# A transformer block on one Trainium2 core: the last matrix product cut into chunks of 3, 3, 3 and 2 tiles

## The chip, the cores and the metric

The kernel runs on one core of one Trainium2 chip. It is timed as device microseconds of one execution. The five engines of the core are called PE (TensorE, the matrix products), DVE (VectorE), ACT (ScalarE), POOL (GpSimd) and SP (SyncE, which here only issues DMAs). Each engine works through its own list of instructions in a fixed order; an instruction that waits holds up everything behind it on the same engine.

## The reference

One layer: banded attention and a Fourier branch in parallel, merged, then a gated ConvFFN. Every sub-layer has an RMS norm before and after it and a residual. The change touches the ConvFFN alone, which is

```python
def conv_ffn(h, w_up, conv_w, conv_b, w_down):
    u, gate = jnp.split(h @ w_up, 2, axis=-1)
    up = jnp.pad(u, ((0, 0), (1, 1), (0, 0)))
    u = up[:, :-2] * conv_w[0] + up[:, 1:-1] * conv_w[1] + up[:, 2:] * conv_w[2] + conv_b
    return (jax.nn.silu(u) * gate) @ w_down
...
x = x + gt2 * rmsnorm(conv_ffn(h2, ...), g_post2)
```

with 1024 tokens, width 1024 and a hidden width of 2816, which is 22 tiles of 128. All is float32.

## The kernel before

**Products.** A float32 operand is split into a rounded high part (an ACT copy) and the rest (a DVE subtraction); a product is then three matmuls (`mm3`: high·high, high·low, low·high). The blocks of a 2x2 block matrix product are formed by Winograd's seven products P1 to P7. A "pair" is one such 2x2 product. Its results collect in three PSUM banks: P1, P6, P7 and P4 run one after another through bank X, P5 and then P3 through Y, P2 in Z. Between P1, P6, P7 and P4 ACT copies X out (`sn`), and the next product into X waits for that copy. P3 adds to Y, so that it waits until what P7's evacuation needs of Y (block 22) has been read by DVE.

**Order.** `wino_items` lists all products ("items") of the stage: for each pair P1, P2, then P4 and P3 of the pair before, then P6, P5, P7. The ConvFFN has 266 items: 22 up pairs (u0 to u21, 84 matmuls each), then 16 down pairs. `run2` walks the list; before the matmuls of item k it emits hooks, `ahead` (loads up to 9 items ahead; high parts 4, low parts 3 items ahead) and `flush` (what was put off to item k by `at_item`). So the place of each instruction on each engine is fixed by these numbers. Item 155 is the product P3 of the last up pair u21, item 156 the P6 of the first down pair d00.

**Down.** The 11 K tiles of each half of w_down are cut into chunks `CH`: 2, 3, 3 and 3 tiles. A chunk has four pairs, one for each m (two token tiles, m and m+4); pair d13 is chunk 1, m = 3. A product of a chunk of 3 is 9 matmuls, of a chunk of 2 it is 6. The sums over chunks stay in SBUF tiles `yd[i, n]`. `d_prep` brings the seven moving operands of the next chunk during the chunk before: w_down loads on SP's queue at items i0-7 to i0+3 (i0 is P1 of the last pair of the chunk before), ACT copies and DVE subtractions from i0-4 on, differences on POOL. The stationary operands of P1, P2 and P4 are stored split by the up stage (`READY`); those of P3, P5, P6 and P7 are stored whole and split in the down stage.

**Evacuation.** In chunks 1 to 3 DVE first adds the bank to the copy (`add(sn, sn, pst)`), and POOL adds the result to `yd`. In the last chunk each finished tile is squared on ACT, gated on POOL (`d_gate`), and with both halves there follow a root on ACT (`rstd_steps`) and a scale and residual on DVE (`d_out`) and the store. The last five products are written out by hand with a chain of its own for each of the last two token tiles.

**Loads.** A load into a two-part operand takes two SBUF tiles of a pool of 40 (`s`); SP waits where a tile is still in use, and each DMA waits for the eighth before it.

Of the kernel before, what the change touches and what calls it, by code (L numbers as in the profile page):

```python
# [16 lines left out]
P = 128  # L17
D = 1024
# [22 lines left out]
def block_kernel(ctx: ExitStack, tc: tile.TileContext, t: dict, out: bass.AP, dbg: dict):  # L41
# [166 lines left out]
    def wino(pairs, items, psf, hooks, FETCH=0):  # L208
# [9 lines left out]
        def do_fetch(j, p):  # L218
            ld, _, nm, _, nk = pairs[j]
            parts = ld[p]  # L220
            names = (f"h{p}_{nm}", f"l{p}_{nm}") if len(parts) == 2 else (f"r{p}_{nm}",)
            ts_ = [s(n, R if len(parts) == 2 else F)[:, :nk * P] for n in names]
            for x, src in zip(ts_, parts):
                load(out=fbits(x) if len(parts) == 2 else x, in_=src)
            st[j][p if len(parts) == 2 else STA[p]] = tuple(ts_) if len(parts) == 2 else ts_[0]
# [1460 lines left out]
    def d_prep(c, jl):  # L1686
# [25 lines left out]
        at(i0 - 7, lambda: ld("11", 0, 0))  # L1712
        at(i0 - 5, lambda: ld("21", 1, 0))
        at(i0 - 4, lambda: ld("12", 0, 1))
        at(i0 - 2, lambda: ld("22", 1, 1))
        at(i0 + 3, lambda: ld("21b", 1, 0))
# [30 lines left out]
    def d_out(i, n, r):  # L1747
        nc.vector.scalar_tensor_tensor(out=yd[i, n], in0=yd[i, n], scalar=r, in1=x1t[i, n], op0=ALU.mult, op1=ALU.add)  # L1748
# [321 lines left out]
```

## Time and profile before

| | us |
|---|---|
| median of 3 runs | 1413.59 (1411.74 to 1414.54) |
| the profiled execution | 1413.6 |
| its span, first to last instruction | 1411.8 |
| PE busy | 1285.2 (91%) |
| DVE busy | 1111.7 (79%) |
| ACT busy | 685.0 (49%) |
| POOL busy | 650.1 (46%) |

A matmul of the stage starts about 0.23 us after the one before it while PE has its full clock of 2.4 GHz, and about 0.43 us after it at 1.2 GHz. "Idle before" in a row of PE is the wait ahead of that matmul, and the arrow names what ended it. A count (x111) in a stretch of 25 us is that of the instructions that lie in it, those at its two edges included.

### The profile page before, as it was taken

How to read it: one execution, taken by the hardware profiler on the slowest of the kernel's cores; microseconds unless marked ns; L12 is line 12 of the kernel's file. 1: busy time of each engine (PE TensorE's matmuls, PEld its weight loads, DVE VectorE, ACT ScalarE, POOL GpSimd, SP SyncE). 2: the span in 40 equal slices, each digit the busy share in tenths (PEclk: the TensorE clock that was granted, in tenths of full speed). 3: DMA queues.
4: the chain of work that ended last, by engine and by line, in shares of the span. 5: the costliest groups of instructions: out<-in, count | busy, mean ns of one | idle time of the engine just before them, and what ended most of it. 6: DMA issues, size and time to landing. Idle time of an engine off the chain costs nothing. (4 is left out here: it accounts for less than half of the span.)

```text
span 1411.8 us, 18488 instructions
## 1 busy us (share of the span) xinstructions
PE 1285.2 (91%) x5840; PEld 1040.8 (74%) x5840; DVE 1111.7 (79%) x1768; ACT 685.0 (49%) x1414; POOL 650.1 (46%) x480
## 2 busy tenths in 40 slices
PE   4769979887999999999987999999999997999995
PEld 3658858666888887778766888888888875777774
DVE  6887999998688897663899986666666696777987
ACT  7555333323566776332755554444544464443442
POOL 1673554554044335430476554444444444364754
PEclk8779999998999999999999999999999999999997
DMA  9714768674614444741622444444344558657563
GB/s 305 220 53 144 227 211 277 199 240 136 201 41 120 123 125 120 233 170 53 189 65 68 134 139 130 119 116 123 108 124 129 153 154 256 213 181 223 164 214 135
DMA packets 253303, 223.63 MB, mean 158 GB/s; under 512 B 15100, under 2 KB 206228, under 8 KB 253204
## 3 DMA queue, kind: packets, MB, share of 16 engines
q1 hardware_dynamic: 253204, 222.44, 51.7%
q8 instruction: 46, 0.75, 0.2%
q14 instruction: 53, 0.43, 0.1%
HBM read 165.49 MB, written 56.62 MB: 157 GB/s over the span
## 5 line engine op out<-in xcount | busy, mean ns | idle before, releaser
L68 DVE TENSOR_TENSOR lP_u<-A_u,hP_u 128x512 fp32r<-128x512 f32 x132 | 103.1, 784 | 43.3 <-ACT hP_u L292 24.4
L354 ACT COPY snP_u<-X_u 128x512 f32<-128x512 f32 x57 | 33.5, 588 | 142.3 <-PE X_u L87 122.9
L68 POOL TENSOR_TENSOR A_u<-A_u,A_u 128x512 f32<-128x512 f32 x44 | 72.3, 1645 | 37.1 <-issue 22.3
L1245 POOL TENSOR_SCALAR p<-p,sm 128x640 f32<-128x640 f32 (+1 forms) x64 | 48.5, 777 | 84.3 <-PE pp L1250 39.2
L68 POOL TENSOR_TENSOR yd<-yd,snP_d 128x512 f32<-128x512 f32 x33 | 52.1, 1579 | 75.7 <-DVE snP_d L68 75.5
L68 POOL TENSOR_TENSOR A_u<-S_u,A_u 128x512 f32<-128x512 f32 x22 | 29.5, 1342 | 102.7 <-DVE lP_u L68 102.4
L292 ACT CAST hP_u<-A_u 128x512 fp32r<-128x512 f32 x121 | 74.6, 619 | 0.9 <-DVE u L68 0.9
L68 DVE TENSOR_TENSOR lP_d<-rP_d,hP_d 128x384 fp32r<-128x384 f32 (+1 forms) x64 | 55.7, 873 | 7.1 <-ACT hP_d L292 6.8
L354 ACT COPY snP_d<-X_d 128x512 f32<-128x512 f32 x46 | 26.8, 584 | 64.3 <-PE X_d L87 55.7
L80 ACT CAST ph<-pp 128x512 fp32r<-128x512 f32 x76 | 44.3, 585 | 22.5 <-PE pp L1250 21.3
L68 DVE TENSOR_TENSOR pl<-pp,ph 128x512 fp32r<-128x512 f32 x76 | 51.6, 680 | 3.1 <-ACT ph L80 2.6
L719 DVE SCALAR_TENSOR_TENSOR acc<-wm,sv,acc 128x512 f32<-128x512 f32 x56 | 51.2, 915 | 1.1 <-DMA wm<-in_w_mod 0.3
L1239 ACT ACTIVATE p<-p,nm 128x640 f32<-128x640 f32 (+1 forms) x64 | 51.3, 802 | 0.7 <-DVE nm L1232 0.7
L1555 POOL TENSOR_SCALAR z<-xr,ry 128x512 f32<-128x512 f32 x15 | 16.7, 1121 | 74.5 <-DVE ry L68 68.0
L1225 DVE CUSTOM_DVE_ANT_0 p<-ss,mask 128x640 f32<-128x640 f32 (+1 forms) x64 | 49.9, 780 | 0.0
L1250 PE MATMUL pp<-ident,p 128*128 128x128 f32 x304 | 46.9, 274 | 3.1 <-POOL p L1245 1.8
L68 POOL TENSOR_TENSOR wd<-wd,wd 128x512 f32<-128x512 f32 x22 | 35.2, 1618 | 27.7 <-DMA wd<-in_w_down 16.1
L68 DVE TENSOR_TENSOR lP_g<-A_g,hP_g 128x512 fp32r<-128x512 f32 x48 | 44.4, 934 | 4.2 <-ACT hP_g L80 3.9
L85 PE MATMUL X_d<-dT,hP_d 128*128 128x512 f32 x88 | 36.5, 414 | 12.0 <-ACT snP_d L354 11.9
L635 ACT ACTIVATE c_g<-c_g 128x512 f32<-128x512 f32 x32 | 19.8, 631 | 56.4 <-DVE c_g L68 48.2
L68 DVE TENSOR_TENSOR u<-Y_u,snP_u 128x512 f32<-128x512 f32 x22 | 15.2, 689 | 39.9 <-PE Y_u L87 39.9
L1250 PEld LDWEIGHTS pp<-ident,p 128*128 128x128 f32 x304 | 37.1, 140 | 12.4 <-POOL p L1245 3.6
(860 smaller groups left out, 4816.1 us busy)
## 6 DMA issues: line engine op xcount, KB each, us to landing
A_u<-in_w_up SPq DMA_DIRECT2D x88, 256.0 KB, 3.8
wm<-in_w_mod SPq DMA_DIRECT2D x66, 256.0 KB, 4.3
wd<-in_w_down SPq DMA_DIRECT2D x55, 256.0 KB, 4.4
A_g<-in_w_in SPq DMA_DIRECT2D x32, 256.0 KB, 5.8
wmc<-in_w_mod SPq DMA_DIRECT2D x32, 256.0 KB, 4.1
ws<-in_w_mod SPq DMA_DIRECT2D x30, 256.0 KB, 6.0
x<-in_x SPq DMA_DIRECT2D x16, 256.0 KB, 5.7
sga_d<-c_g SPq DMA_DIRECT2D x16, 256.0 KB, 3.5
```

What stands on the lines that cost most here:

```text
L68: return (eng or nc.vector).tensor_tensor(out=out, in0=a, in1=b, op=op)
L80: copy(hi, src)
L85: nc.tensor.matmul(ps, ah, bh, start=start, stop=False, skip_group_check=True)
L292: copy(st[j]["half", p][0], st[j][STA[p]])
L354: copy(d["s" + p], d["X"])
L635: nc.scalar.activation(out=d, in_=d, func=AF.Sigmoid)
L719: nc.vector.scalar_tensor_tensor(out=accs[g], in0=wmt[i], scalar=sv[:, o:o + 1], in1=accs[g], op0=ALU.mult, op1=ALU.add)
L1225: nc.vector.tensor_tensor_reduce(out=p_, in0=ssc[:, lo:768], in1=self.mk, op0=ALU.add, op1=ALU.max, scale=1.0, scalar=-3.0e38, accum_out=s ...
L1239: nc.scalar.activation(out=self.pt[g], in_=self.pt[g], func=AF.Exp, scale=SCALE, bias=self.m[:, g:g + 1], accum_out=self.sm[:, g:g + 1])
L1245: nc.gpsimd.tensor_scalar(out=self.pt[g], in0=self.pt[g], scalar1=self.sm[:, g:g + 1], scalar2=1.0, op0=ALU.mult, op1=ALU.mult)
L1250: nc.tensor.transpose(pp[:, g * P:(g + 1) * P], self.pt[g][:, j * P:(j + 1) * P], ident)
L1555: eng.tensor_scalar(out=zn[tk, h], in0=xr[tk][h], scalar1=ry[tk, 1], scalar2=1.0, op0=ALU.mult, op1=ALU.mult)
```

## The change

It has five parts. (1) The chunks are 3, 3, 3 and 2 tiles. (2) w_down is asked for at items i0-10 to i0+1; two-part loads are issued 6 items ahead, not 9, and for a chunk of 2 both parts share one tile. (3) For the last chunk all seven stationary operands are stored split: the up stage splits P3, P5, P6 and P7 of its tiles 9, 10, 20 and 21 (four ACT copies and four DVE subtractions each for tiles 20 and 21). (4) In chunks 1 to 3 POOL adds the copy `sn` to `yd` first, and DVE then adds the bank to `yd`; what P7 evacuates of Y comes two items after P7, not one, in the up stage too. (5) The end by hand is gone; the last two token tiles share one chain of a root, and stores stand one item later.

```diff
-                    if i <= k + FETCH and (j, p) not in seen["l"]:
+                    if i <= k + (9 if len(pairs[j][0][p]) == 1 else 6) and (j, p) not in seen["l"]:
...
                 if p in ("P1", "P6", "P7"):
                     d["s" + p] = s(f"sn{p}_{nm}")
                     copy(d["s" + p], d["X"])
+                    if ready(j):
+                        at_item(k + 1, lambda ev=ev, q={"P1": 11, "P6": 12, "P7": 22}[p], x=d["s" + p]: ev(q, None, x))
...
-                    at_item(k + 1, lambda d=d, ev=ev, q=q: ev(q[0], d[q[1]], d.get(q[2])))
+                    at_item(k + (2 if p == "P7" else 1), lambda d=d, ev=ev, q=q: ev(q[0], d[q[1]], d.get(q[2])))
...
-    CH = [(0, HF % 3)] + [(c, 3) for c in range(HF % 3, HF, 3)]
+    CH = [(c, min(3, HF - c)) for c in range(0, HF, 3)]
...
+    def split_early(c, p):
+        return p in ("P1", "P2", "P4") or c == len(CH) - 1
...
-            return lambda: (op(d, a, b, nc.gpsimd), [(1, lambda: g_store(f, p, d))])[1]
+            return lambda: (op(d, a, b, nc.gpsimd), [(2, lambda: g_ready(f, p, d)) if early else (1, lambda: g_store(f, p, d))])[1]
...
-        at(i0 - 7, lambda: ld("11", 0, 0))
...
-        at(i0 + 3, lambda: ld("21b", 1, 0))
+        at(i0 - 10, lambda: ld("11", 0, 0))
...
+        at(i0 + 1, lambda: ld("21b", 1, 0))
...
             y = yd[i, n]
-            if sn is None:
-                add(y, y, pst)
-            else:
-                add(sn, sn, pst)
-                add(y, y, sn, None if last and m == NT // 2 - 1 else nc.gpsimd)
+            if pst is None:
+                add(y, y, sn, nc.gpsimd)
+                if last and q == 11:
+                    x1_load(m)
+                    x1_load(m + NT // 2)
+                return None
+            add(y, y, pst)
             return finish(i, n) if last else None
...
-        run(14, M - 5)
...
+        run(14, M)
...
+        v, sq, r, n1 = (tiny(f"{n}dl", 2, 8) for n in ("v", "sq", "r", "n1"))
+        add(v, ssd[:, i0::NT // 2, 0], ssd[:, i0::NT // 2, 1])
```

DVE ahead of item 155, before: `lP4_u21` and `lP3_u21` are the low parts that items 154 and 155 need, `gg21<-Y_u21` is the read of Y that item 155 waits for, `tb10` the convolution of tile 10.

```order
L68 TENSOR_TENSOR lP4_u21_10918<-A22_u21_10510,hP4_u21_10917 128x512
L1626 SCALAR_TENSOR_TENSOR tb10_10922<-u0_7464,vec_67,tb10_10922 128x1024
L1627 SCALAR_TENSOR_TENSOR tb10_10922<-u0_7464,vec_67,tb10_10922 128x1024
L68 TENSOR_TENSOR dT201_10909<-dT201_10854,dT200_10908 128x512
L68 TENSOR_TENSOR lP3_u21_10946<-A12_u21_10508,hP3_u21_10945 128x512
L68 TENSOR_TENSOR gg21_10979<-Y_u21_10924,snP7_u21_10963 128x512
```

The same place now, from `glP720` (a low part for the last chunk; `glP520`, another, stands between it and `lP4_u21`):

```order
L68 TENSOR_TENSOR glP720_10938<-gg9_10467,ghP720_10937 128x512
L1639 SCALAR_TENSOR_TENSOR tb10_10940<-u0_7468,vec_67,tb10_10940 128x1024
L1640 SCALAR_TENSOR_TENSOR tb10_10940<-u0_7468,vec_67,tb10_10940 128x1024
L68 TENSOR_TENSOR dT201_10925<-dT201_10868,dT200_10924 128x512
L68 TENSOR_TENSOR lP3_u21_10962<-A12_u21_10512,hP3_u21_10961 128x512
L68 TENSOR_TENSOR glP620_10966<-gf9_10523,ghP620_10965 128x512
L68 TENSOR_TENSOR dT101_10987<-wd0000_10539,dT100_10986 128x512
L68 TENSOR_TENSOR dT201_10925<-dT202_10869,dT200_10924 128x512
L68 TENSOR_TENSOR lP6_d00_10994<-rP6_d00_10839,hP6_d00_10993 128x384
L68 TENSOR_TENSOR gf10_10880<-gf10_10880,tb10_10940 128x512
L68 TENSOR_TENSOR gg10_10817<-gg10_10817,tb10_10940 128x512
L68 TENSOR_TENSOR gg21_11035<-Y_u21_10942,snP7_u21_10984 128x512
```

Between `lP4_u21` and `gg21<-Y_u21` stood four instructions of DVE, and twelve stand there now.

SP around the first w_down tile of chunk 1 (`wd1000`), before (`g_d3P60` and `g_d3P30` store what POOL makes of the last up pair, `hP1_d03` is a load for pair d03):

```order
L224 DMA hP1_d03_11204<-g_d0P10_6616 128x256
L224 DMA lP1_d03_11205<-g_d0P11_6617 128x256
L1594 DMA g_d3P60_6654<-gf10_10864 128x4x128
L224 DMA hP2_d03_11217<-g_d0P20_6618 128x256
L224 DMA lP2_d03_11218<-g_d0P21_6619 128x256
L1594 DMA g_d3P30_6650<-gf21_11040 128x4x128
L1669 DMA wd1000_11233<-in_w_down 128x512
```

And now:

```order
L232 DMA hP2_d02_11215<-g_d0P20_6618 128x384
L232 DMA lP2_d02_11216<-g_d0P21_6619 128x384
L224 DMA rP6_d02_11219<-g_d0P60_6624 128x384
L232 DMA hP4_d01_11242<-g_d0P40_6621 128x384
L232 DMA lP4_d01_11243<-g_d0P41_6622 128x384
L224 DMA rP5_d02_11246<-g_d0P50_6623 128x384
L1682 DMA wd1000_11265<-in_w_down 128x512
L1682 DMA wd1001_11267<-in_w_down 128x512
L1682 DMA wd1002_11269<-in_w_down 128x512
L224 DMA rP7_d02_11271<-g_d0P70_6625 128x384
L1605 DMA g_d3P20_6648<-ghP221_11225 128x4x128
```

The loads of chunk 1's w_down now stand ahead of all stores that wait for the last up pair.

DVE in the last chunk, where pair d32 gives bank Y to its P3, before (`yd10`, `yd11` are the outputs of a token tile finished earlier, `snP7_d32` the copy of P7):

```order
L68 TENSOR_TENSOR r2d1_13077<-rd1_13075,n1d1_13076 128x1
L1748 SCALAR_TENSOR_TENSOR yd10_11157<-yd10_11157,r2d1_13077,xf10_12859 128x512
L1748 SCALAR_TENSOR_TENSOR yd11_11319<-yd11_11319,r2d1_13077,xf11_12861 128x512
L68 TENSOR_TENSOR snP7_d32_13113<-snP7_d32_13113,Y_d32_13078 128x512
L68 TENSOR_TENSOR lP6_d33_13117<-rP6_d33_13003,hP6_d33_13116 128x384
L68 TENSOR_TENSOR lP5_d33_13143<-rP5_d33_13020,hP5_d33_13142 128x384
L68 TENSOR_TENSOR snP1_d33_13139<-snP1_d33_13139,Z_d33_13152 128x512
```

And now:

```order
L68 TENSOR_TENSOR r2d1_13108<-rd1_13106,n1d1_13107 128x1
L1761 SCALAR_TENSOR_TENSOR yd10_11231<-yd10_11231,r2d1_13108,xf10_12903 128x512
L1761 SCALAR_TENSOR_TENSOR yd11_11446<-yd11_11446,r2d1_13108,xf11_12905 128x512
L68 TENSOR_TENSOR yd61_11535<-yd61_11535,Y_d32_13110 128x512
L68 TENSOR_TENSOR yd30_11564<-yd30_11564,Z_d33_13173 128x512
L68 TENSOR_TENSOR yd60_11586<-yd60_11586,X_d32_13018 128x512
L68 TENSOR_TENSOR yd21_11602<-yd21_11602,Y_d32_13110 128x512
```

The splits are gone from the last chunk, and the read of Y now writes `yd61`, to which POOL has to have added `snP7_d32` before.

## Rows read from the trace of the kernel before

**Rows 1.** The page: the span.

```profile
span 1411.8 us, 18488 instructions
```

**Rows 2.** Busy time by stretch: PE, PEld, DVE, ACT, POOL, clock, DMA share, GB/s.

```profile
1150.00:1175.00 25.00, 23.04 (x100) 18.21 (x99) 24.81 (x35) 15.66 (x30) 7.57 (x6) 1.00 0.49 143
1175.00:1200.00 25.00, 18.00 (x65) 13.62 (x63) 13.21 (x18) 8.62 (x19) 8.86 (x7) 0.86 1.01 309
1200.00:1225.00 25.00, 21.56 (x82) 17.16 (x83) 22.40 (x30) 14.01 (x29) 8.68 (x6) 0.86 0.66 204
1225.00:1250.00 25.00, 25.00 (x111) 20.41 (x110) 11.89 (x20) 7.32 (x16) 8.84 (x6) 1.00 0.74 236
1250.00:1300.00 50.00, 48.64 (x210) 38.77 (x209) 42.52 (x47) 21.92 (x44) 29.33 (x18) 1.00 0.59 183
1300.00:1350.00 50.00, 46.82 (x202) 37.38 (x202) 44.38 (x48) 22.26 (x46) 30.74 (x20) 1.00 0.60 188
1350.00:1400.00 50.00, 43.30 (x173) 33.19 (x172) 42.09 (x74) 18.67 (x49) 29.71 (x22) 0.94 0.54 180
```

**Rows 3.** PE's waits from 1130 to 1412: in total, times, longest.

```profile
PE X_d L85 <- ACT snP_d L354: 12.1, 7, 5.9
```

**Rows 4.** PE in order of time: start, us, instruction, idle before.

```profile
1154.70 0.50 PE L85 MATMUL Y_u<-B22a,hP_u 128*128 128x512 f32 x1 [0.92 <-DVE gg L68]
...
1157.60 0.39 PE L85 MATMUL X_d<-dT,hP_d 128*128 128x512 f32 x1
...
1164.48 0.39 PE L85 MATMUL X_d<-dT4n,hP_d 128*128 128x512 f32 x1
...
1186.95 0.80 PE L85 MATMUL X_d<-dT,hP_d 128*128 128x512 f32 x1 [5.88 <-ACT snP_d L354]
...
1192.94 0.39 PE L87 MATMUL Z_d<-dB,lP_d 128*128 128x512 f32 x1
...
1395.27 0.80 PE L85 MATMUL X_d<-dT4n,hP_d 128*128 128x512 f32 x1 [5.24 <-ACT snlP L1957]
...
1401.92 0.40 PE L87 MATMUL Y_d<-dB,lP_d 128*128 128x512 f32 x1
```

**Rows 5.** ACT in order of time, at the first long wait of PE.

```profile
1184.62 0.62 ACT L1697 CAST dB<-wd 128x512 fp32r<-128x512 f32 x1 [8.71 <-DMA wd<-in_w_down]
```

**Rows 6.** SP's issues in order of time, chunk 1's first w_down tiles.

```profile
1179.69 1.62 SPq L1669 DMA_DIRECT2D wd<-in_w_down  x3
```

**Rows 7.** DVE in order of time, at the end of the up stage.

```profile
1136.69 0.69 DVE L68 TENSOR_TENSOR lP_u<-A_u,hP_u 128x512 fp32r<-128x512 f32 x1
1137.29 1.78 DVE L68 TENSOR_TENSOR glP<-gf,ghP 128x512 fp32r<-128x512 f32 x1
1139.00 1.77 DVE L68 TENSOR_TENSOR glP<-gg,ghP 128x512 fp32r<-128x512 f32 x1
...
1153.96 0.68 DVE L68 TENSOR_TENSOR gg<-Y_u,snP_u 128x512 f32<-128x512 f32 x1
```

**Rows 8.** POOL in order of time, in the same stretch.

```profile
1136.85 1.68 POOL L68 TENSOR_TENSOR wd<-wd,wd 128x512 f32<-128x512 f32 x1 [1.41 <-DVE dB L68]
...
1148.70 1.74 POOL L68 TENSOR_TENSOR dT<-wd,dT 128x512 f32<-128x512 f32 x1
```

**Rows 9.** Groups of the last chunk, 1326 to 1400: busy, mean ns, idle before.

```profile
L68 POOL TENSOR_TENSOR yd<-yd,G 128x512 f32<-128x512 f32 x14 | 19.3, 1391 | 9.7 <-ACT jd L1742 9.7
L68 POOL TENSOR_TENSOR yd<-yd,snP_d 128x512 f32<-128x512 f32 x12 | 18.5, 1538 | 16.9 <-DVE snP_d L68 16.9
L1748 DVE SCALAR_TENSOR_TENSOR yd<-yd,r2d,xf 128x512 f32<-128x512 f32 x12 | 10.5, 918 | 0.4
L1742 ACT ACTIVATE jd<-yd 128x512 f32<-128x512 f32 x14 | 8.8, 630 | 26.9 <-POOL yd L68 25.3 <-DVE yd L68 1.5
L141 ACT ACT_TABLE_LOAD x1 | 1.3, 1283 | 0.0
```

**Rows 10.** DVE in order of time, at the end.

```profile
1406.79 2.08 DVE L1748 SCALAR_TENSOR_TENSOR yd<-yd,r2dl,xf 128x512 f32<-128x512 f32 x3 [0.27 <-DVE r2dl L68]
```

More of the change, by code (lines that the diff above doesn't have):

```diff
@@ L206, in wino_items, with wino @@
         return items
-    def wino(pairs, items, psf, hooks, FETCH=0):
+    def wino(pairs, items, psf, hooks, slots=False):
         st = [dict() for _ in pairs]
@@ L220, in do_fetch @@
             parts = ld[p]
[L221 to L225, printed above, removed]
+            w = nk * P
+            if len(parts) == 1:
+                st[j][STA[p]] = s(f"r{p}_{nm}")[:, :w]
+                load(out=st[j][STA[p]], in_=parts[0])
+                return
+            if 2 * w <= 512:
+                both = s(f"b{p}_{nm}", R)
+                st[j][p] = both[:, :w], both[:, w:2 * w]
+            else:
+                st[j][p] = s(f"h{p}_{nm}", R)[:, :w], s(f"l{p}_{nm}", R)[:, :w]
+            for x, src in zip(st[j][p], parts):
+                load(out=fbits(x), in_=src)
         def do_load(j, keys=("A11", "A21", "A12", "A22")):
@@ L1711, in d_prep @@
         first = c == 0
[L1712 to L1716 removed]
+        at(i0 - 10, lambda: ld("11", 0, 0))
+        at(i0 - 8, lambda: ld("21", 1, 0))
+        at(i0 - 7, lambda: ld("12", 0, 1))
+        at(i0 - 5, lambda: ld("22", 1, 1))
+        at(i0 + 1, lambda: ld("21b", 1, 0))
         for k in range(nk):
@@ L1736, in y_tile @@
     def y_tile(i, n):
-        if len(yd) < 5:
+        if len(yd) < 3:
             return s(f"yd{i}{n}")
-        return miscD[0].tile([P, 512], F, tag="yd", name=f"yd{i}{n}", bufs=11)
+        return miscD[0].tile([P, 512], F, tag="yd", name=f"yd{i}{n}", bufs=13)
     def d_square(i, n):
@@ L1745, in d_gate, with d_out, d_store @@
         mul(yd[i, n], yd[i, n], G2[n], nc.gpsimd)
-    def d_out(i, n, r):
-        nc.vector.scalar_tensor_tensor(out=yd[i, n], in0=yd[i, n], scalar=r, in1=x1t[i, n], op0=ALU.mult, op1=ALU.add)
+    def d_out(i, n, r, y=None):
+        nc.vector.scalar_tensor_tensor(out=yd[i, n], in0=yd[i, n] if y is None else y, scalar=r, in1=x1t[i, n], op0=ALU.mult, op1=ALU.add)
+    def d_store(i, n):
         store(out=out[i * P:(i + 1) * P, n * 512:(n + 1) * 512], in_=yd[i, n])
@@ L1758, in down_pair @@
         ld = {p: [d[m] for d in g_d[c, p]] for p in STA}
+        half = set()
         def finish(i, n):
+            first = i not in half
+            half.add(i)
+            if not first and m == NT // 2 - 1:
+                return None
             def squares():
@@ L1764, in squares @@
                 d_gate(i, n)
-                if (i, 1 - n) not in x1t:
-                    x1_load(i)
+                if first:
                     return None
                 rs = rstd_steps(ssd[:, i, :], f"d{i}")
-                return [(1, rs[0]), (2, lambda: [rs[1](), d_out(i, 0, rs[2]), d_out(i, 1, rs[2])] and None)]
+                return [(1, rs[0]), (2, lambda: [rs[1](), d_out(i, 0, rs[2]), d_out(i, 1, rs[2])] and None),
+                        (3, lambda: [d_store(i, h) for h in range(2)] and None)]
             return [(1, squares)]
@@ L1812, in load_g2 @@
             load(out=G2[h], in_=gt_d[1, :, h * 512:(h + 1) * 512])
-    at(pos[NF - 1, "P3"] + 8, swap_misc)
+    at(pos[NF - 1, "P3"] + 6, swap_misc)
     at(pos[NF + 12, "P1"], load_g2)
-    run, ahead, flush, due, pre, conv, sums, mm, evac, st = wino(pairs, items, ps, hooks, 9)
+    run, ahead, flush, due, pre, conv, sums, mm, evac, st = wino(pairs, items, ps, hooks, True)
     with tc.manual_schedule():
```

70 lines of the change are left out of this document (27 added, 43 removed).

## The prediction

> **What bounds the kernel now.** The page first: a span of 1411.8 us [rows 1]. The profiled execution took 1413.6, so 1.8 us lie around the span; the median of the runs, 1413.59, is the same. Then the busy times by stretch [rows 2]: 25 undisturbed us hold 111 matmuls, 1150 to 1225 holds 247 of 333, the two stretches of 50 us after 1250 hold 210 and 202 of 222, the last 173. The reader is to see that PE sets the time and that these holes are what can be won. PE's waits [rows 3] name their main releaser: ACT copying a bank out, 12.1 us in 7 waits. PE in order of time [rows 4] gives the places, 5.88 us before 1186.95 and 5.24 before 1395.27, and PE's pace: 30 matmuls in the 6.88 us from 1157.60 to 1164.48, 0.229 each. Right after the 5.88 of idling, 14 matmuls take the 5.99 us from 1186.95 to 1192.94: the clock is at 1.2 and not at 2.4 GHz, as the granted share of 0.86 in that stretch also says [rows 2], and that costs 2.8 us more.
>
> From item 156 (1157.60) to the end of the last matmul (1401.92 + 0.40 = 1402.32) there are 912 matmuls: 156 left of chunk 0, and 3 chunks of 252. At 0.229 they are 208.8 us and took 244.7, so 35.9 are lost: about 18.5 between chunks 0 and 1, 7.3 at the two later seams (12 and 20 matmuls missing), the rest in the last chunk. The last 9.5 us up to 1411.8 are a tail without PE.
>
> **The change part by part.** *w_down earlier.* Chunk 1's first w_down is asked for at 1179.69 [rows 6], behind stores that wait for the last up pair. ACT's first cast of it waits 8.71 us for the DMA and runs at 1184.62 [rows 5]; ACT does nothing else meanwhile, so the copy of bank X behind it comes late and PE waits its 5.88 us. After the change these loads stand ahead of all those stores, and the products beside them last 2.06 us (9 matmuls) and not 1.37. I count this stall, its half clock and the small waits that follow as gone: of 18.5 lost, 2 stay (0.5 within chunk 0, 1.5 at the seam). What is late next is the bank Y of the last up pair:
>
> *P7's evacuation two items after P7.* Item 155 writes Y and can't start before DVE has done `gg21<-Y_u21`. Before it waited 0.92 us for that [rows 4] (1153.96 to 1154.56 [rows 7]). Now 12 and not 4 DVE instructions stand between `lP4_u21` and it. I count DVE from 1137.29, with the order now: 21 instructions at the spacing of 0.60 that a 128x512 has alone (1136.69 to 1137.29 [rows 7]), two convolution steps, about 2.5, and a split of 128x384, about 0.47: 15.6 us. Then POOL works at the same time: 1137.29 to 1139.00 is 1.71 and not 0.60 [rows 7], while POOL's operation takes 1.68 [rows 8]. In the old order 9.1 us of DVE work took 17.3 (1137.29 to the end of `gg21`), with 8 POOL operations in it, the first at 1136.85 and the last at 1148.70 [rows 8]: 8.2 more, about 1.05 for each. Chunk 0 now has a third K tile and so 12 of them there: 12.6 us more. 15.6 + 12.6 puts the end of `gg21` at 1165.5. PE would be ready about 1155.0 plus the 6 matmuls by which two products have grown, 1156.4: it idles 9 to 10 us, and then I take the half clock as after the 5.88, 2.8 us. Item 156 starts at 1165.6 + 2.7 (12 matmuls) + 2.8 = 1171.1, 13.5 later than before. Bounds: without POOL's toll DVE is through at 1152.9 and PE waits for nothing; with every one of the 21 at 1.71 it is 1177. I take the middle because it is the toll that the same stretch paid.
>
> The Trainium skill, page "SBUF — State Buffer", section "Who interferes with whom", says that a DVE instruction with two SBUF inputs contends with a GpSimd instruction that reads SBUF, and that the one that issues first has the shared ports for its whole length while the other fully blocks. The trace agrees that both slow down together [rows 7, 8], but by 1.05 for each POOL operation. If DVE paid a whole undisturbed one, 1.39 [rows 9], 12 x 0.34 = 4 us would be added and the sum below would be 1410.7 us.
>
> *POOL adds first in chunks 1 to 3.* P3 now waits for DVE's add of Y, and that for POOL's add of the copy, where a POOL add takes 1.54 [rows 9] and POOL also makes the next chunk's differences. The seams of later chunks lose 7.3 now; their w_down comes earlier, but POOL is ahead of DVE: I take 2.5 and 2.0. Bounds 0 and 5 each.
>
> *The last chunk.* A pair is 42 matmuls, 9.6 us. POOL has 4 gates at 1.391 and 3 adds at 1.538 in it, 10.2 us [rows 9]. That alone would cost 0.6 a pair. The chain is longer: P3's end is T; the read of Y 0.7, the square 0.8 [rows 9], the gates one after another; the first outputs come at T + 3.2, under POOL's work about T + 5.5. The second token tile's root follows on ACT, and P7's copy stands behind it, about T + 7.1; P4 then starts at T + 7.7 where PE could at T + 6.9, and Y is read by T + 11.6, so that the next P3 ends near T + 13.1 and not T + 9.6. I take 3 us for each of 3 pairs and 1.3 for a table load [rows 9]: 10.5. The splits that are gone from this chunk are on DVE and ACT, which have room. Bounds: 1.8, POOL's length alone, to 13.
>
> *The end.* The 5.24 before 1395.27 [rows 4] came from a copy behind a root that waited for DVE in the chain written by hand; both are gone. Of the tail of 9.5, the 4.5 from the last matmul to 1406.79 [rows 10] hold one scale and residual of the other tile, 0.92 [rows 9]; without it 3.55. Then four at 0.69 instead of three [rows 10], 2.76, and 1411.8 - 1408.87 = 2.9 for store and end: 9.2.
>
> Sum: 1171.1 + 906 matmuls (6 of chunk 0 are in the 1156.4) at 0.229 = 207.5, + losses 0.5 + 1.5 + 2.5 + 2.0 + 10.5 = 17, + tail 9.2 = 1404.8 of span, + 1.8 = **1406.6 us**, 7 less than before. The gain is 19 us of losses, the price 13.5; with losses of 24 instead of 17 it is nil.
>
> **The rivals.** (A) The forecast; with its losses between 12 and 23 its own range is 1401 to 1412. (B) *Bank Y is free sooner.* POOL's differences wait for w_down, as before 1136.85 (1.41 of idling [rows 8]); where POOL pauses DVE runs at 0.60. Then PE idles some 4 us and keeps its clock: item 156 at 1156.4 + 4 + 2.7 = 1163.1, so 8 less, about 1398.6. Against it: POOL had no pause in the busy 12 us before [rows 8]. (C) *Slower: the coupling POOL, DVE, PE.* Since DVE's read of Y waits for POOL's add, any POOL backlog reaches PE, in the last chunk above all. Pairs of 14.5 us, 4.9 lost on each of three, and 5 at each later seam, with a half clock after one wait (2.8), make the losses 0.5 + 1.5 + 10 + 14.7 + 1.3 + 2.8, about 31: 1420.6. It decides from 24 on. For it: POOL's 10.2 against PE's 9.6. Against: the gates could already start while P5 and P3 run. (D) *The loads come no earlier.* SP waits for a free tile of the 40 ahead of w_down and the 5.88 with its 2.8 stays, on top of the price at item 155: 1415.3. Against it: the loads are now cut to one tile or asked for later, which frees tiles. (E) *The last chunk is bound by POOL's length alone:* 4 lost, not 10.5: 1400. For it: DVE and ACT have fewer instructions in it.
>
> **How the numbers follow.** A 0.45, B 0.18, C 0.16, E 0.12, D 0.09. The predicted time is A's. 0.2%, 2.8 us, is about what a measurement of this kernel can tell from no change: faster than 1410.8 are B, E and some seven tenths of A (0.62); A's upper end and a part of D are within (0.22); slower than 1416.4 are C less its mild end, and the rest of D (0.16). The range leaves out one in ten on each side: below, B and E together (1392); above, the worse half of C (1418).
>
> **What would show it.** Right: PE waits 9 to 10 us before the first matmul of u21's P3, for DVE's `gg`, and the next 14 matmuls take near 6 us; no wait of over 2 between chunks 0 and 1, and ACT's casts of `dB` no longer end on a DMA; in the last chunk waits for DVE's `yd` of 2 to 3 us a pair and P3 to P3 about 13; 9.2 us behind the last matmul. Wrong: a wait under 6 at item 155 (B), pairs near 10 (E) or over 14 (C), or a cast of `dB` that still waits over 5 us for w_down (D).

## The result and the profile after

The changed kernel takes 1420.68 us (median of 18 runs) beside 1414.2 for the kernel before; the ratio is 1.0047 (95% interval 1.0034 to 1.0059), 6.6 us slower. Forecast were 1406.6 us and a range of 1392 to 1418: wrong, in sign too. The profiled execution took 1421.2 us, its span 1419.5.

PE's waits of the changed kernel, in total, times and longest, answer to [rows 3]:

```profile
PE Y_u L85 <- DVE gg L68: 10.6, 1, 10.6
PE Y_d L85 <- DVE yd L68: 9.5, 5, 2.7
PE X_d L85 <- ACT snP_d L361: 7.7, 4, 3.5
PE X_u L85 <- ACT snP_u L361: 1.9, 1, 1.9
PE Z_d L85 <- DMA hP_d<-g_d0P: 0.3, 1, 0.3
```

The wait foreseen before u21's P3 is there, and the waits for ACT's copies have given way to waits for DVE's `yd`. Where they lie, PE in order of time:

```profile
1150.90 0.50 PE L85 MATMUL X_u<-T3a,hP_u 128*128 128x512 f32 x1 [1.88 <-ACT snP_u L361]
1171.62 0.79 PE L85 MATMUL Y_u<-B22a,hP_u 128*128 128x512 f32 x1 [10.65 <-DVE gg L68]
...
1219.26 0.50 PE L85 MATMUL Y_d<-dB,hP_d 128*128 128x512 f32 x1 [1.43 <-DVE yd L68]
1285.19 0.50 PE L85 MATMUL X_d<-dT,hP_d 128*128 128x512 f32 x1 [1.61 <-ACT snP_d L361]
1296.25 0.50 PE L85 MATMUL Y_d<-dB,hP_d 128*128 128x512 f32 x1 [2.62 <-DVE yd L68]
1375.12 0.50 PE L85 MATMUL X_d<-dT4n,bP_d 128*128 128x512 f32 x1 [1.90 <-ACT snP_d L361]
1379.52 0.79 PE L85 MATMUL Y_d<-dB,bP_d 128*128 128x512 f32 x1 [2.23 <-DVE yd L68]
1390.18 0.50 PE L85 MATMUL X_d<-dT4n,bP_d 128*128 128x512 f32 x1 [0.62 <-ACT snP_d L361]
1394.58 0.50 PE L85 MATMUL Y_d<-dB,bP_d 128*128 128x512 f32 x1 [2.75 <-DVE yd L68]
1403.92 0.79 PE L85 MATMUL X_d<-dT4n,bP_d 128*128 128x512 f32 x1 [3.54 <-ACT snP_d L361]
1407.34 0.50 PE L85 MATMUL Y_d<-dB,bP_d 128*128 128x512 f32 x1 [0.49 <-DVE yd L68]
...
1408.61 0.39 PE L87 MATMUL Y_d<-dB,bP_d 128*128 128x512 f32 x1
```

Busy time by stretch, with the columns of [rows 2]:

```profile
1150.00:1175.00 25.00, 13.45 (x51) 10.52 (x52) 23.77 (x26) 15.12 (x27) 13.51 (x9) 0.80 0.63 185
1175.00:1200.00 25.00, 25.00 (x111) 20.50 (x110) 21.87 (x32) 14.54 (x27) 6.02 (x4) 1.00 0.73 219
1200.00:1225.00 25.00, 23.31 (x101) 18.43 (x100) 19.87 (x23) 11.49 (x23) 11.32 (x8) 1.00 1.02 335
1225.00:1250.00 25.00, 25.00 (x111) 20.50 (x110) 20.20 (x28) 12.38 (x25) 8.27 (x6) 1.00 0.78 254
1250.00:1300.00 50.00, 45.77 (x193) 36.74 (x192) 40.44 (x42) 18.66 (x37) 28.10 (x18) 0.98 0.50 159
1300.00:1350.00 50.00, 50.00 (x217) 40.73 (x216) 35.92 (x43) 18.15 (x37) 22.27 (x16) 0.99 0.66 211
1350.00:1400.00 50.00, 42.51 (x174) 33.22 (x172) 38.13 (x61) 20.40 (x50) 32.70 (x25) 0.93 0.65 205
```

The hole between chunks 0 and 1 is nearly closed (65 and 82 matmuls in its two worst stretches before, 101 in the worst now), and the one at item 155 has opened instead: 51. The seam between chunks 1 and 2 (193, before 210) is worse, the next one full, the last chunk no better (174, before 173).

From P6 of one pair to P6 of the next an undisturbed pair of 63 matmuls takes 14.45 us, one of 42 takes 9.62. Item 156 starts at 1175.87 and the last matmul ends at 1409.00; the surplus of the pairs is 2.3 us between chunks 0 and 1, 6.4 at the next seam (5.6 and 0.85), nothing at the third, 16.7 in the last chunk (6.45, 4.2 and 6.05 from its second pair on). That is 25.5 us of losses, and a tail of 10.5. Counted the same way, the kernel before loses 17.9 us up to the P6 of d10 (the first pair of chunk 1), 2.3 and 1.7 at its two later seams, and 13.6 in its last chunk. Below, these pair by pair surpluses, each from one profiled execution, are what the kernels are compared by.

### The profile page after: what moved, and what is told of

It reads as the page before. It is cut to its first block, busy times and chain, and to the rows that moved or that the text cites. A ratio compares the mean times of both kernels' runs of the same rounds, so it can differ in the third digit from the quotient of the medians.

```text
span 1419.5 us, 18505 instructions
## 1 busy us (share of the span) xinstructions
PE 1283.9 (90%) x5840; PEld 1039.8 (73%) x5840; DVE 1107.7 (78%) x1754; ACT 683.6 (48%) x1405; POOL 638.8 (45%) x481
## 5 line engine op out<-in xcount | busy, mean ns | idle before, releaser
L68 DVE TENSOR_TENSOR lP_d<-rP_d,hP_d 128x384 fp32r<-128x384 f32 x48 | 44.7, 931 | 12.7 <-ACT hP_d L299 12.4
L68 DVE TENSOR_TENSOR u<-Y_u,snP_u 128x512 f32<-128x512 f32 x22 | 15.2, 690 | 41.2 <-PE Y_u L87 41.1
L1259 PEld LDWEIGHTS pp<-ident,p 128*128 128x128 f32 x304 | 37.1, 140 | 12.2 <-POOL p L1254 3.4
L68 POOL TENSOR_TENSOR gs<-gg,gg 128x512 f32<-128x512 f32 x11 | 14.7, 1339 | 68.6 <-ACT snP_u L361 41.5
```

What stands on the lines that cost most here:

```text
L68: return (eng or nc.vector).tensor_tensor(out=out, in0=a, in1=b, op=op)
L1259: nc.tensor.transpose(pp[:, g * P:(g + 1) * P], self.pt[g][:, j * P:(j + 1) * P], ident)
```

## The experiments

All were timed beside the kernel before. "Faster than the changed kernel by x" is the difference of the two ratios to before times 1414 us.

**What the new evacuation costs, and what the order in the last chunk costs, place by place.**

*P7's evacuation one item after P7 again, in the up stage.*

```diff
-at_item(k + (2 if p == "P7" else 1), ...)
+at_item(k + (2 if p == "P7" and ready(j) else 1), ...)
```

> The changed kernel, but in the up stage what P7 evacuates of Y comes one item after P7 again. Theory (P7's later evacuation in the up stage): DVE's gg21 is then 5 instructions earlier, which took 3.9 us in the changed kernel (1166.95 to 1170.89), so the wait of 10.65 us before u21's P3 shrinks to 6 to 7 us, the 1.4 us wait at 810 goes, and the whole is 5 to 7 us faster than the changed kernel (1414 to 1416, the same as before). Rival (DVE is simply behind at this place, because chunk 0 has a third K tile and the last chunk's operands are split there): the wait stays over 9 us and the time within 2 us of the changed kernel's 1420.7.

1414.7 us, ratio 1.0006 (0.9995 to 1.0016): 5.8 us faster than the changed kernel, as the theory had it. PE before u21's P3:

```profile
1165.14 0.79 PE L85 MATMUL Y_u<-B22a,hP_u 128*128 128x512 f32 x1 [5.20 <-DVE gg L68]
```

Half of the 10.65 goes with the second item. A wait of 1.4 us early in the up stage, which I had not looked for, is gone too.

*The evacuation of chunks 0 to 2 as before, the last chunk as changed.*

```diff
+at_item(k + (2 if p == "P7" and (j < NF or j >= NF + 12) else 1), ...)
...
-                add(y, y, sn, nc.gpsimd)
+                if last:
+                    add(y, y, sn, nc.gpsimd)
...
-            add(y, y, pst)
+            if last or sn is None:
+                add(y, y, pst)
+            else:
+                add(sn, sn, pst)
+                add(y, y, sn, nc.gpsimd)
```

> The changed kernel, with the evacuation of chunks 0 to 2 as before: P7's one item later, DVE adds the bank to the copy, POOL the result to yd; the up stage and the last chunk as changed. Theory (the loss of 6.4 us between chunks 1 and 2 comes from the new evacuation alone: the kernels with the old one lose 2.2 there): 6.4 falls to 2 to 3 us, 3.5 to 4.5 us faster than the changed kernel, 1416 to 1417.5. Rival (it comes from DVE being slowed by POOL's differences in that stretch, whichever adds first: the run with DVE first still lost 3.7): 3.5 or more stay, under 3 us faster, 1418 to 1420.

1414.93 us, ratio 1.0009 (0.9997 to 1.0021): 5.4 us faster than the changed kernel, more than the theory's 4.5. The seam between chunks 1 and 2 loses 2.2 and not 6.4, and the one between 0 and 1 nothing. In the profiled execution, 2.9 us above the median, the last chunk, which is as in the changed kernel, lost 3.8 more, with a granted clock of 0.87 in it and not 0.90. The stretch of the seam has the 210 matmuls of before again:

```profile
1250.00:1300.00 50.00, 48.69 (x210) 38.72 (x209) 38.44 (x43) 21.31 (x42) 27.95 (x18) 1.00 0.50 159
```

*DVE first, POOL second, in all chunks, P7 still two items late.*

```diff
-add(y, y, sn, nc.gpsimd)
...
-add(y, y, pst)
+if sn is None:
+    add(y, y, pst)
+else:
+    add(sn, sn, pst)
+    add(y, y, sn, nc.gpsimd)
```

> The changed kernel, but DVE adds the bank to the copy first and POOL adds the result to yd, as before. Theory (DVE's read of Y waits for POOL's add): the 2.62 us wait for yd between chunks 1 and 2 goes, in the last chunk the waits for yd (2.2, 2.75) shrink under 1 us, and the down stage loses some 8 us less: 1411 to 1414. Rival (what holds DVE is its own list: outputs and the root's small steps, slowed by POOL, stand ahead of its read of Y): the last chunk still loses 14 us or more and the time stays within 3 us of 1420.7.

1421.89 us, ratio 1.0055 (1.0039 to 1.0072): no gain, the rival. It is a sum of two signs. The seams lose 5.5 instead of 8.7 (between chunks 1 and 2 PE waits 1.89 us and not 1.61 and 2.62), but the last chunk 19.5 instead of 16.7, and the tail is 12.2. So at the seam it matters who adds first, and in the last chunk who adds first is not what PE waits for.

*In the down stage the read of Y first, and in the last chunk the outputs behind the other tile's root.*

```diff
-return [(1, rs[0]), (2, lambda: [rs[1](), d_out(i, 0, rs[2]), d_out(i, 1, rs[2])] and None),
-        (3, stores)]
+return [(1, rs[0]), (2, lambda: [rs[1]()] and None),
+        (3, lambda: [d_out(i, 0, rs[2]), d_out(i, 1, rs[2])] and None), (4, stores)]
...
+due.setdefault(k, []).insert(0, fn)    # for P7's read of Y in the down stage
```

> The changed kernel; in chunks of the down stage DVE's read of Y after P7 stands first among what is due in its item, and in the last chunk the two outputs of a token tile come one item later, behind the root of the other token tile. Theory (in the last chunk the root, and behind it on ACT the copy of X, waits for outputs that wait for POOL's gates; then the read of Y waits for the outputs): the waits of 1.90, 2.23, 2.75 and 3.54 us in the last chunk fall to under 1 us each and the half clocks with them, 6 to 9 us faster than the changed kernel: 1412 to 1415. Rival (POOL's work itself, 10.2 us a pair against PE's 9.6, sets the pace): POOL's adds come just as late, the waits stay over 1.5 us, under 2.5 us faster: 1418 to 1421.

1414.95 us, ratio 1.0008 (0.9996 to 1.0020): 5.5 us faster than the changed kernel, just short of the theory's 6. The last chunk loses 12.5 instead of 16.7; the waits for ACT's copy there fall from 6.1 to 1.8 (the other 1.6 of the row below is at the seam between chunks 1 and 2), those for `yd` hardly:

```profile
PE Y_u L85 <- DVE gg L68: 10.8, 1, 10.8
PE Y_d L85 <- DVE yd L68: 9.6, 5, 3.0
PE X_d L85 <- ACT snP_d L364: 3.4, 2, 1.8
```

*No gates in the last chunk.*

```diff
-d_gate(i, n)
...
```

> The changed kernel without the multiplication by the gate in the last chunk (it leaves that part of the computation out, and with it 16 POOL operations of 128x512). Theory (POOL's gates are what the outputs, and through them DVE, ACT and PE, wait for, and what slows DVE's own instructions): the last chunk's loss of 16.7 us falls to 4 to 7 and the tail of 10.5 by 1 to 1.5: 1409 to 1412. Rival (the chain is long by its order, roots and outputs ahead of the copies and reads, whatever POOL does): half or less of that, 1415 to 1419.

1416.83 us, ratio 1.0016 (1.0001 to 1.0031): 4.4 us faster than the changed kernel, in the rival's window. An output is back at 909 ns (1300 in the changed kernel) and the tail at 8.8 us, but the last chunk still loses 15.2 of 16.7 us, with waits of 2.5 to 2.7 for `yd`. In that execution, 2.6 us above the median, PE's waits in the last chunk sum to 8.9 us, where they sum to 11.5 in the changed kernel and to 7.9 with the order of the run above; a granted clock of 0.88 and not 0.90 takes back nearly half of what that gives. So the gates have a part in the waits, as the order has, and neither is the whole.

*Both mends, and all three* (the second line of the diff; with it go the lines of the run on chunks 0 to 2).

```diff
+(front if ready(j) and p == "P7" else at_item)(k + (2 if p == "P7" and ready(j) else 1), ...)
...
+(front if p == "P7" and j >= NF + 12 else at_item)(k + (2 if p == "P7" and j >= NF + 12 else 1), ...)
```

> The changed kernel with both mends: P7's evacuation one item later in the up stage as before, and in the down stage the read of Y first and the outputs behind the other root. Theory (two separate causes, 6.0 us and 5.7 us): they add up, 1408 to 1410, faster than before by 0.3 to 0.4%. Rival (what is won at the end of the up stage is lost again, since DVE and POOL are then the bound of the down stage): 1412 to 1415.

1411.61 us, ratio 0.9979 (0.9966 to 0.9992): 9.6 us faster than the changed kernel, of 11.3 that the two gave alone; between theory and rival.

> The changed kernel with all three mends: P7's evacuation one item later in the up stage; the evacuation of chunks 0 to 2 as before; in the last chunk the read of Y first and the outputs behind the other root. One by one they gave 5.8, 5.4 and 5.5 us. Theory (three independent prices of the new evacuation): 15 us or nearly so, 1404 to 1407. Rival (they overlap, what one wins the next wait takes back): 1408 to 1412.

1406.81 us, ratio 0.9946 (0.9934 to 0.9959): 14.3 us faster than the changed kernel, of 16.7. The three gains nearly add up. That the time is the 1406.6 us of the forecast is chance: this is not the change that was forecast, PE waits 5.2 us at item 155 and not 9 to 10, and the last chunk loses 12.8 us and not 10.5. Two of the three mends take the new evacuation back; the third is a new order, since the kernel before has its outputs ahead of the read of Y too.

**The early splits.**

```diff
-    return p in ("P1", "P2", "P4") or c == len(CH) - 1
+    return p in ("P1", "P2", "P4")
```

> The changed kernel, but the last chunk's operands of P3, P5, P6 and P7 are stored whole again and split in the down stage. Theory (the extra splits crowd DVE at the end of the up stage): three splits of 1.7 us each no longer stand ahead of gg21, so the wait of 10.65 falls to about 5.5, while the last chunk takes back 16 splits of 128x256 at about 0.4 us, some of them in front of DVE's read of Y, which costs 1 to 3 us: 1416 to 1419. Rival (the splits are hidden in both places): the wait stays near 10 and the time near 1420.7; if the splits are dear in the last chunk, over 1423.

1418.43 us, ratio 1.0039 (1.0024 to 1.0055), 1.1 us faster than the changed kernel, as the theory had it but not clear of the intervals. The wait before u21's P3 is 7.10 and not 10.65, the seam between chunks 0 and 1 loses nothing (2.3 with the splits; but nothing either in the run with the old evacuation in chunks 0 to 2, which keeps them), and the last chunk takes back 4.7. The splits are dear in the up stage and nearly worth it in the last chunk.

**The chunks and the requests of w_down.**

*The requests alone, in the kernel before.*

```diff
-at(i0 - 7, lambda: ld("11", 0, 0))
+at(i0 - 10, lambda: ld("11", 0, 0))
...
```

> The kernel before, with one thing of the change alone: w_down is asked for at the new items, i0-10 to i0+1. Theory (the stall between chunks 0 and 1 was only that request, standing behind stores): PE's wait of 5.88 us and the half clock after it go, 8 to 10 us faster than before: 1404 to 1406. Rival (SP still waits for free tiles ahead of w_down, or the earlier loads hold up those of the stationary operands): under 3 us faster, 1411 to 1416.

1409.63 us, ratio 0.9969 (0.9959 to 0.9979): 4.4 us faster than before, half of the theory. ACT's cast no longer waits for w_down, and yet the stall of PE has not moved (what is gained lies behind it, where the loss of the next pair falls from 7.8 us to 4.3); ACT, in order of time:

```profile
1186.38 0.58 ACT L354 COPY snP_d<-X_d 128x512 f32<-128x512 f32 x1 [7.53 <-DMA g_d3P<-gf]
```

and PE:

```profile
1187.02 0.80 PE L85 MATMUL X_d<-dT,hP_d 128*128 128x512 f32 x1 [5.84 <-ACT snP_d L354]
```

Before, ACT waited 8.71 us for w_down [rows 5] and PE 5.88 [rows 4]; now the same copy waits for a store of the up stage to land.

*With two-part loads 6 items ahead.*

```diff
-if i <= k + FETCH and (j, p) not in seen["l"]:
+if i <= k + (9 if len(pairs[j][0][p]) == 1 else 6) and (j, p) not in seen["l"]:
```

> The kernel before with the whole of the second part: w_down at the new items, and two-part loads 6 items ahead and not 9. The run with the early requests alone kept a wait of 5.84 us there: ACT's copy of bank X was ended by a store of the last up pair, which I read as a copy that waits for one of the 40 tiles. Theory (tiles run out): loads issued later hold fewer tiles, the copy gets one at once, and the wait falls under 2 us: 1402 to 1406. Rival (it is not the number of tiles but the store itself, which is late, or the loads that now come late in their turn): the wait stays over 4 us, 1408 to 1411.

1406.57 us, ratio 0.9944 (0.9926 to 0.9961): 7.9 us faster than before with the second part of the change alone (all but the shared tile for a chunk of 2). The time lies between theory and rival, the wait is the rival's: the copy isn't held, but PE is, now by a load:

```profile
1186.96 0.79 PE L85 MATMUL X_d<-dB,hP_d 128*128 128x512 f32 x1 [5.35 <-DMA hP_d<-g_d0P]
```

*The same loads 8 items ahead* (in the kernel of the run with the outputs later, below).

```diff
-(9 if len(pairs[j][0][p]) == 1 else 6)
+(9 if len(pairs[j][0][p]) == 1 else 8)
```

> The fastest kernel so far (1405.5), with two-part loads 8 items ahead and not 6. Its wait of 5.2 us between chunks 0 and 1 is for a load of P1's two parts that was issued in time but landed 6 us later, with the DMA engines full. Theory (the bytes are the bound: the DMA engines are busy 94 to 98% there, whatever comes first): the wait goes to another load, store or tile and the time stays within 2 us, 1404 to 1408. Rival (it is the order of the requests): the wait falls under 2 us, 4 to 6 us faster, 1399 to 1402.

1405.6 us, ratio 0.9938 (0.9924 to 0.9951), no change, as the theory had it. PE waits for the copy once more, and that for the store; the DMA share of 1175 to 1200 is 1.00:

```profile
1185.63 0.80 PE L85 MATMUL X_d<-dT,hP_d 128*128 128x512 f32 x1 [4.15 <-ACT snP_d L354]
```

```profile
1175.00:1200.00 25.00, 18.60 (x71) 13.95 (x69) 18.57 (x23) 9.26 (x20) 10.75 (x8) 0.91 1.00 311
```

Four orders of the same requests, and each has 4 to 6 us of wait, for w_down, a store, a load, a store. The losses up to d10's P6 are 17.9, 13.8, 10.8 and 13.9 us: the order is worth up to 7 in these single executions (the last is 2.1 us above its median), and over 10 remain in each. That the bytes set these is read from the DMA share and not shown: a kernel that moves fewer was not tried, and the changed kernel, with a share of 1.02 at this seam, loses only 2.3.

*The chunks alone, in the kernel before.*

```diff
-    CH = [(0, HF % 3)] + [(c, 3) for c in range(HF % 3, HF, 3)]
+    CH = [(c, min(3, HF - c)) for c in range(0, HF, 3)]
```

> The kernel before with the chunks 3, 3, 3, 2 alone; w_down is asked for at the old items. Theory (the stall between chunks 0 and 1 came from a first chunk that is too short for the stores of the last up pair and for w_down): with 4 x 4.8 us more before chunk 1 the 5.88 us wait goes without any earlier request, while the third K tile puts three more instructions of DVE and three POOL differences ahead of gg21, 2 to 4 us of wait before u21's P3: 1405 to 1411. Rival (the request itself is late): a wait of 4 us or more stays between chunks 0 and 1, ended by a DMA of w_down: 1413 to 1418.

1414.5 us, ratio 1.0000 (0.9989 to 1.0010): no difference: the time is the rival's, the mechanism the theory's. The stall between chunks 0 and 1 is gone with the old requests (2.3 us lost there) and u21's P3 waits 2.79 us; the last chunk takes the gain, 21.6 us, with waits of 1.98 and 5.28 at the end.

**The end, and the best kernel.**

*The kernel before with the second part, and what is due at the last P7 behind its copy.*

```diff
-        flush(M - 3)
         mm(M - 3)
         d_copy("P7")
+        flush(M - 3)
```

> The kernel before with the whole second part (the run that took 1406.6), and in the end by hand what is due at the last P7 is emitted behind ACT's copy of P7 and not ahead of its products. Theory (the 5.2 us wait before the last P4 comes from the order on ACT alone, a root that waits for DVE ahead of the copy): the wait and the half clock after it go, 5 to 8 us less: 1399 to 1402. Rival (the root is only put off, and the tail without PE grows by as much): 1404 to 1407, with a tail of 12 or more instead of 9.2.

1405.7 us, ratio 0.9943 (0.9931 to 0.9956): as the run without it (0.9944). The 5.23 became 1.52, and a new wait took its place, PE:

```profile
1384.77 0.50 PE L85 MATMUL X_d<-dT4n,hP_d 128*128 128x512 f32 x1 [1.52 <-ACT snlP L1957]
1390.94 0.79 PE L85 MATMUL Y_d<-dB,hP_d 128*128 128x512 f32 x1 [3.84 <-DVE yd L68]
```

Neither theory nor rival: the tail stayed 9.2. The copy was the first of two, DVE's read of Y the second.

*And the outputs one item later.*

```diff
-return [(1, rs[0]), (2, lambda: [rs[1](), d_out(i, 0, rs[2]), d_out(i, 1, rs[2])] and None)]
+return [(1, rs[0]), (2, lambda: [rs[1]()] and None), (3, lambda: [d_out(i, 0, rs[2]), d_out(i, 1, rs[2])] and None)]
```

> As the run with the other order at the end, and in the last chunk the two outputs of a token tile one item later, behind the other tile's root. Theory (outputs ahead of the root hold ACT's copy in this kernel too): the wait of 2.0 us in the last chunk's second pair and the half us around the others go, 1 to 4 us less than that run. Rival (with chunks of 3 last, PE's 14.4 us a pair leaves room for that chain, and outputs one later only come closer to the end): within 1 us of it.

1405.48 us, ratio 0.9941 (0.9928 to 0.9955), the rival: nothing.

*Chunks 2, 3, 3, 3, with two mends and with three.*

```diff
-    CH = [(c, min(3, HF - c)) for c in range(0, HF, 3)]
+    CH = [(0, HF % 3)] + [(c, 3) for c in range(HF % 3, HF, 3)]
```

> The same as the run with both mends, but with the chunks 2, 3, 3, 3. Theory (a first chunk of 3 costs at u21's P3, where DVE and POOL make its third K tile, and a last chunk of 2 leaves PE only 9.6 us a pair for 10.2 us of POOL): the wait before u21's P3 falls under 3 us and the last chunk loses under 8, though some 5 us between chunks 0 and 1 come back, where the DMA engines are full: 1402 to 1406. Rival (what the short first chunk loses there is as much as it saves): 1407 to 1412.

1407.98 us, ratio 0.9957 (0.9942 to 0.9972), in the rival's window: the last chunk loses only 1.6 us, but u21's P3 waits 3.91 and the seam between 1 and 2 still loses 6.3, which the run on the seam then explained.

> The same as the run with the three mends, but with the chunks 2, 3, 3, 3. Theory (with the evacuation mended the order of the chunks is worth little: what it saves between chunks 0 and 1 it pays at u21's P3 and in a last chunk too short for POOL): within 3 us of that run. Rival (the last chunk of 2 is the dearer part): 4 to 7 us faster than that run, 1399 to 1402.

1403.43 us, ratio 0.9930 (0.9918 to 0.9943): the fastest of all, 9.9 us under the kernel before. Against the three mends with 3, 3, 3, 2 it is 2.3 us faster, within the theory's 3, with intervals that overlap. The sum hides two large terms. Up to d10's P6 it loses 10.3 us where the other loses 0.7, but item 156 comes 9.3 us earlier (1.4 of it six fewer matmuls), and the last chunk, now of three tiles, loses 3.9 us and not 12.8. From the last chunk's first P6 to the last matmul, first with 3, 3, 3, 2, then with 2, 3, 3, 3 (the columns are those of [rows 2]):

```profile
1346.34:1394.86 48.52, 40.48 (x157) 30.65 (x155) 42.23 (x69) 20.16 (x51) 36.49 (x26) 0.91 0.66 214
1331.87:1389.36 57.49, 54.83 (x235) 43.43 (x233) 46.28 (x74) 20.87 (x51) 38.20 (x27) 1.00 0.78 263
```

## Why the prediction was wrong

The sum was 14.6 us of span short. The step that failed most is the size of the last chunk's loss (16.7 us for 10.5); next, the start of DVE's list ahead of item 155, which I took from the kernel before and which came 6.8 us later; then the seam between chunks 1 and 2.

*The bound and the price at item 155: right, but not the start.* The wait was 10.65 us (9 to 10 forecast), ended by `gg`. DVE took from 1144.05 (the first `glP` of the list that I had counted from 1137.29) to 1171.57, 27.5 us, for the work that I had at 28.2. The rows from the third split on, DVE:

```profile
1165.27 1.76 DVE L68 TENSOR_TENSOR glP<-gf,ghP 128x512 fp32r<-128x512 f32 x1
...
1168.62 1.75 DVE L68 TENSOR_TENSOR gf<-gf,tb 128x512 f32<-128x512 f32 x1
1170.29 0.68 DVE L68 TENSOR_TENSOR gg<-gg,tb 128x512 f32<-128x512 f32 x1
1170.89 0.68 DVE L68 TENSOR_TENSOR gg<-Y_u,snP_u 128x512 f32<-128x512 f32 x1
```

The half clock behind it cost 1.5 (12 matmuls in 4.25 us), not 2.8. Item 156 was still 4.8 us later than forecast, 1175.87 and not 1171.1, because the list began at 1144.05 and not at the 1137.29 of [rows 7]. Of these 6.8 us PE was 1.65 behind before the ConvFFN began, where both kernels hold the same products, and the up stage waited 1.4 more; the latter is P7's two items again (it is gone in the run that undoes them). The largest part is a wait of DVE itself, just ahead of the list, which stood in the sum at nothing (the row puts it down to a cast by ACT; what it hung on was not tried):

```profile
1143.44 0.69 DVE L68 TENSOR_TENSOR lP_u<-A_u,hP_u 128x512 fp32r<-128x512 f32 x1 [3.18 <-ACT dB L1710]
```

It falls to 1.20 in the run that undoes P7's two items. The late start goes with a first chunk of 3: the list begins at 1142.13 with the chunks alone, and at 1137.11 in the fastest kernel, with chunks 2, 3, 3, 3. The wait of 1.88 is a copy that waits for DVE, and it too stands in every kernel with a first chunk of 3 (2.0 with the chunks alone); I had not looked at ACT's copies ahead of item 155.

*w_down earlier: the right sum by chance, for a wrong reason.* I took the 5.88 us for a late request. The loss at this seam fell to 2.3 (2.0 forecast), but the requests alone left a wait of 5.84, and the chunks alone, with the old requests, took it away. The DMA engines are full there, a share of 1.01 in [rows 2] that I had passed over, and a third K tile in chunk 0 gives the same stores and loads 4 x 4.8 us more. The longer first chunk is shown by a run; that the full DMA engines are why it helps is argued. I read the releaser of one wait as its cause.

*POOL adds first: failed by its size.* Price at the two later seams together 4.5 forecast (2.5 and 2.0), measured 6.4 and 0. I had counted by stretches of 50 us and put 7.3 at these seams in the kernel before; pair by pair it is 4.0, and what I missed there lies in its last chunk. The run with the old evacuation shows the cause of the 6.4: it is back at 2.2. With DVE first alone the waits there fall from 4.23 to 1.89 us, so most of it is POOL's turn ahead of DVE. Of the 6.4 another 1.7 are half clock behind the wait of 2.62 (18 matmuls in 5.85 us, from 1296.25 on), which I had counted nowhere in these losses. That part is not there in every execution. The 5 us behind this wait in the changed kernel, then the 5 us behind the same wait, 2.58 long, in the run with P7 one item later in the up stage, which changes nothing at this seam:

```profile
1296.25:1301.25 5.00, 5.00 (x15) 3.94 (x16) 5.00 (x9) 0.00 (x0) 0.00 (x0) 0.66 0.58 182
1291.36:1296.36 5.00, 5.00 (x22) 4.10 (x23) 5.00 (x9) 0.49 (x2) 0.00 (x0) 1.00 0.59 178
```

The second execution loses 4.7 at this seam, under the 5 by which I had bounded it.

*The last chunk: the step that failed most, by its size,* 16.7 us and not 10.5. The mechanism was the forecast's own chain, outputs, root, copy, read of Y. One size that was missing is again the half clock, 1.65 us behind the wait of 2.23 and 1.6 behind that of 3.54 (the granted clock of 1350 to 1400 is 0.93). Another is the pace of DVE's outputs. DVE in the second pair:

```profile
1370.79 3.31 DVE L1761 SCALAR_TENSOR_TENSOR yd<-yd,r2d,xf 128x512 f32<-128x512 f32 x2
1374.02 0.15 DVE L68 TENSOR_TENSOR vd<-ssd 128x1 f32<-128x1 f32 x1
...
1375.26 1.18 DVE L68 TENSOR_TENSOR r2d<-rd,n1d 128x1 f32<-128x1 f32 x1
1376.48 2.38 DVE L1761 SCALAR_TENSOR_TENSOR yd<-yd,r2d,xf 128x512 f32<-128x512 f32 x2
1378.79 0.68 DVE L68 TENSOR_TENSOR yd<-yd,Y_d 128x512 f32<-128x512 f32 x1
```

and ACT, whose copies stand behind that root:

```profile
1374.39 0.20 ACT L141 ACTIVATE sqd<-vd 128x1 f32<-128x1 f32 x1 [3.91 <-DVE vd L140]
1374.50 1.05 ACT L361 COPY snP_d<-X_d 128x512 f32<-128x512 f32 x2
```

Two outputs take 3.31 us and two more 2.38, where two took 1.8 in [rows 9], since POOL works beside them more of the time: the mean of an output went from 918 ns to 1300. So the read of Y came at 1378.79. The small multiplication of the root went from 304 to 812, but the small steps of the roots together took no longer (the others of them meet POOL less): 12.3 us for six token tiles, 12.8 before. What the gates and the slower outputs are worth the run without gates shows: 1.5 us of the loss, 2.7 of the waits. What the order does, the run that changes it: 4.2 of the 16.7 us. With all three mends 12.8 remain, and 3.9 when the last chunk has three tiles. So most of the loss comes with a pair of 42 matmuls, 9.6 us, which is too short for this chain; which link of it holds PE longest I leave open.

*The end: 10.5 us and not 9.2.* The small steps of the last root met POOL's last gates; without the gates the tail is 8.8.

Together: 1404.8 + 4.8 (item 156) + 8.5 (losses of 25.5 for 17) + 1.3 (tail) = 1419.4 us, the span being 1419.5. My point of break-even was 24, and the losses passed it. Rival C had the place, a half clock and the time, 1420.6; I gave it 0.16 because the gates could start while P5 and P3 run. The time is in part luck: C took 31 us of losses, 25.5 were measured, and the late start of item 156 and the longer tail, which it did not have, make up the rest. Its mechanism, POOL's backlog reaching PE through the add, is there at the seam but not shown in the last chunk, which loses 19.5 us with DVE first and 15.2 without the gates. B, D and E fell: PE waited its full 10 us, no cast waited long for w_down, the pairs were far from POOL's own 10.2 us.

## What to carry to other kernels

A wait's last releaser need not be its cause: in a stretch where the DMA share was about 1, the same requests in four orders kept 4 to 6 us of stall, and more work ahead of it, a longer first chunk, took it away. A new wait of 2 to 4 us can cost a half clock too, 1.5 to 1.7 us here, or nothing. Where a bank's read stands behind other work of DVE, its place in the list counts: five instructions fewer ahead of it took 5.45 us off PE's wait at item 155. A change in five parts is summed with signs: the requests and the load rule alone were worth 7.9 us, taking the new evacuation back and one new order in the last chunk gave 14.3, and both lay under one number. The chunks of 3, 3, 3 and 2 alone changed nothing, and in two mended kernels chunks 2, 3, 3, 3 were 3.1 and 2.3 us faster, with intervals that overlap.

## What the runs showed of the hardware

Instructions of DVE that touch almost no data can take as long as one of POOL's. DVE in the tail of the changed kernel:

```profile
1410.51 0.72 DVE L68 TENSOR_TENSOR vdl<-ssd 128x2 f32<-128x2 f32 x1 [0.79 <-ACT jd L1755]
1411.26 1.19 DVE L1988 TENSOR_SCALAR vdl<-vdl 128x2 f32<-128x2 f32 x1
...
1412.93 0.16 DVE L68 TENSOR_TENSOR n1dl<-rdl 128x2 f32<-128x2 f32 x1
```

and POOL there:

```profile
1409.94 1.27 POOL L68 TENSOR_TENSOR yd<-yd,G 128x512 f32<-128x512 f32 x1
1411.16 1.26 POOL L68 TENSOR_TENSOR y<-yd,G 128x512 f32<-128x512 f32 x1
```

A step on 128x2 takes 1.19 us while POOL's gate runs, and one of the same size 0.16 once it is done. The Trainium skill, page "SBUF — State Buffer", section "Who interferes with whom", has a DVE instruction with two SBUF inputs contend with one of POOL's that reads SBUF, and the one that issues second fully blocked; the root's multiplication of 1.18 us above, on 128x1, agrees. The 1.19 us is a step with one tensor operand, for which the page allows it only in some modes; the trace does not show which mode it ran in. At the end of the up stage the toll was 0.94 us for each POOL operation, less than the whole of one: 27.5 us, less 15.6 of DVE's own work (the forecast's estimate) and 1.6 of idling, over 11 operations.

A wait of PE of the same length is followed by a half clock in one execution and not in another: at the seam between chunks 1 and 2 the granted clock was 0.66 over the 5 us behind 2.62 us of idling, and 1.00 behind 2.58.
